# Sample rows of a hybrid decoder step: attention and state products in halves of 64 columns, and one state update for eight rows

## The chip, the cores and the metric

One Trainium2 chip, of which the kernel uses one core. The metric is the device time of one launch in microseconds (us). A core has a matrix engine (PE, whose weight loads are listed apart as PEld), a vector engine (DVE), a scalar engine (ACT), GpSimd (POOL) and a queue engine (SP) from which nearly all of this kernel's DMAs are issued. Each engine works through its own instructions in order.

## What is computed

One trunk layer for a prompt of 2048 tokens and for a sample batch of 8 rows with 8 new tokens each (64 sample tokens). The layer is: RMSNorm, one input projection, two groups of heads side by side, one output projection, then a squared-ReLU MLP. All inputs are float32. What matters here are the two sample parts:

```python
def swa_window(q, k_all, v_all, sinks):           # 8 q heads, 2 kv heads, head size 64
    scores = jnp.einsum('bqhgd,bkhd->bhgqk', qg, k_all) * (HEAD_DIM ** -0.5)
    p = sink_softmax(scores, mask, sink)          # 128 cached keys + the new ones
    out = jnp.einsum('bhgqk,bkhd->bqhgd', p, v_all)

def step(S, xs):                                  # GLA, 4 heads, dk 64, dv 128
    qd, kd, vv, ab = xs
    o = jnp.einsum('bthk,bhkv->bthv', qd, S)      # the state's read-out
    S = ab[..., None] * S + jnp.einsum('bthk,bthv->bhkv', kd, vv)
```

For the sample batch the scan has one step: all 8 new tokens of a row form one chunk. The state `S` of a row and head is 64 x 128, so that two heads (a head group `g`) fill 128 partitions.

## The kernel before

**Stages.** The kernel projects the attention columns and does the attention tile by tile (16 prompt tiles of 128 tokens, then the sample tile, whose index is `NB` = 16), then the GLA part tile by tile, then the output projection, then the MLP. The columns of the GLA part are projected by `projecting` (products `gproj`, each 128 x 128 weights with 384 moving columns), which serves as fill: the loops draw a given number of its products between the steps of the latency-bound work, so that PE always has something in its queue.

**Sample attention** (`sample_unit`, line 564). There are four units, one for each half `c` of the sample rows and each kv head `r`. A unit makes scores `sc` (128 rows: 4 sample rows x 4 heads x 8 tokens; 192 columns: 128 cached keys and the 64 new ones), the softmax in the tile `s` (tag `ss`, two buffers), two transposes into `pt`, two copies by DVE into `pc`, and the product with the values into the bank `av`: one product with the new values `vals[NB]` (64 partitions, 128 moving columns) and four with the cached values (32 moving columns each). Each uses all 128 columns of the values, that is of both kv heads, and only the half `av[rr]` of the result that belongs to head `r` is copied out. `vals[NB]` is written in `take_rest` (line 362).

**Sample GLA** (`gla_sample`, line 1306). It is a generator, called `side` in the main loop, and takes one step whenever the GLA loop over the prompt tiles (`gla`, line 1214) yields: five turns for each prompt tile, from tile 1 on. The part that matters is the last one. It first makes the inner product `oi` (four products, 128 columns of the values, 64 moving columns). Then for each head group `g`:

- the read-out `oe`: 8 products, one for each row `b`, whose weights are the state `s0[:, b]` (128 x 128) and whose moving operand has 16 columns;
- the decay of the state: one DVE multiplication over 128 x 1024 elements;
- the update, in four steps of two rows each (`b2`), each a turn of the side generator: two masked copies of the keys (`s_kx`, one for each row, by DVE), then a yield, then four products of 64 x 64 weights and 128 moving columns into a bank `ds`, and one DVE addition of 256 columns to the state;
- the state is written out by a DMA; after the first group the state of the second is loaded into the same place, and the generator passes `S_WAIT[1]` = 6 turns.

After the second group it transposes and normalizes the result (`finish_out`), and frees the pool `ss`; then `split_wo` (line 1425), which prepares the output weights in eight steps, one for each prompt tile, takes its place.

**PSUM.** `bank` (line 178) gives the kinds `a`, `b` and `c` two buffers each, `d` and `e` one. All of the side generator's products go to kind `b`.

**Records.** A float32 product that is not a transpose appears in the trace as two matmul records (with two weight loads), so the 8 products of one group's read-out are 16 records. A transpose, and a product of the type fp32r (`gproj`), is one record. The instructions of each engine need not stand in the order of the source: the first masked copies of the keys, for instance, stand far ahead of the read-out.

Of the kernel before, what the change touches and what calls it, by code (L numbers as in the profile page):

```python
# [12 lines left out]
F32 = mybir.dt.float32  # L13
# [3 lines left out]
ALU = mybir.AluOpType  # L17
# [4 lines left out]
P = 128  # L22
D = 1024
KT = D // P
T = 2048
NB = T // P
DB, DT = 8, 8
NS = DB * DT
W = 128
HD = 64  # L30
# [13 lines left out]
SL = len(S_LEVELS)  # L44
# [108 lines left out]
def hybrid_step_kernel(ctx: ExitStack, tc: tile.TileContext, I, O):  # L153
    nc = tc.nc
# [18 lines left out]
    te, ac, dv = (InOrder(tc, engine) for engine in (nc.tensor, nc.scalar, nc.vector))  # L173
# [4 lines left out]
    def bank(shape, kind, name):  # L178

        return ps.tile(shape, F32, tag=kind, name=name, bufs=1 if kind in "de" else 2)  # L180
# [21 lines left out]
    ident = cpool.tile([P, P], F32, name="ident")  # L202
# [79 lines left out]
    sp = open_pool("a_s")  # L282
    gxTs, ropes, xs_in, xTs, proj, qks, rots, heads, vals = {}, {}, {}, {}, {}, {}, {}, {}, {}
# [69 lines left out]
    def scaled(out, i, src):  # L353
        ac.activation(out, src, AF.Copy, scale=rstd_all[: rows(i), i : i + 1])
# [7 lines left out]
    def take_rest(i):  # L362

        n = rows(i)
        p_ = proj.pop((i, 1))
        w = 640 - A_N
        scaled(qks[i].rearrange("p h d -> p (h d)")[:n, A_N:640], i, p_[:n, :w])
        vps = p_[:n, w : w + P]
        rs = rstd_all[:n, i : i + 1]
        gps_ = p_[:n, w + P : A_N]  # L370
        ranks = glr[:n, i // 2, i % 2, :48].rearrange("p (a r) -> p a r", a=3)
        scaled(ranks[:, 0:3:2], i, gps_.unsqueeze(1).to_broadcast([n, 2, 16]))

        def low(out, src, hi):
            dv.scalar_tensor_tensor(out, src, rs, f32(hi), op0=ALU.mult, op1=ALU.subtract)

        if i == NB:
            vals[i] = vn = sp.tile([NS, P], F32, tag="vv", name="vn", bufs=4)
            scaled(vn, i, vps)
            return lambda: low(ranks[:, 1], gps_, ranks[:, 0])  # L380
        vals[i] = vv = sp.tile([P, 2, 2, HD], F32R, tag="vv", name=f"vv_{i}", bufs=4)
        vh, vl = vv[:, :, 0, :], vv[:, :, 1, :]
        src = vps.rearrange("p (r d) -> p r d", r=2)
        scaled(vh, i, src)
        if i == NB - 1:
            vo = sp.tile([P, P], F32, tag="kc", name="vo", bufs=1)
            scaled(vo, i, vps)
            stores.append((O["v_win_prompt"][0, 0].rearrange("w h d -> w (h d)"), vo))

        def lows():  # L390
            low(vl, src, vh)
            low(ranks[:, 1], gps_, ranks[:, 0])

        return lows
# [26 lines left out]
    half_of = slice(HD), slice(HD, P)  # L421
# [142 lines left out]
    def sample_unit(c, r, cached, kcs, mo):  # L564

        yield
        qs, kns = heads[NB]
        rr = slice(r * HD, (r + 1) * HD)
        if r == 0:
            pc = bank([P, 4, P], "d", f"pc_{c}")  # L570
            for b in range(4):
                te.transpose(pc[:, b, :], cached["k", c][:, b, :], ident)
            kcs[c] = sp.tile([P, 4, P], F32, tag="kc", name=f"kc_{c}", bufs=1)
            ac.activation(kcs[c], pc, AF.Copy)
        kc = kcs[c]
        yield
        sc = bank([P, W + NS], "b", f"ssc_{r}_{c}")
        for b4 in range(4):
            b = c * 4 + b4
            lq = qs[rr, b].rearrange("p j t -> p (j t)")  # L580
            o_ = slice(b4 * 32, b4 * 32 + 32)
            te.matmul(sc[o_, :W], lq, kc[rr, b4, :], start=True, stop=True)
            te.matmul(sc[o_, W:], lq, kns[rr, :], start=True, stop=True)
        s = sp.tile([P, W + NS], F32, tag="ss", name=f"ss_{r}_{c}", bufs=2)
        m = sp.tile([P, 1], F32, tag="sm", name=f"sm_{r}_{c}", bufs=2)
        yield
        dv.tensor_tensor_reduce(
            s, sc, smask[:, c, :], scale=1.0, scalar=sinkp[:, r : r + 1], op0=ALU.add, op1=ALU.max, accum_out=m
        )
        neg = sp.tile([P, 1], F32, tag="sneg", name=f"sneg_{r}_{c}", bufs=2)  # L590
        dv.tensor_scalar(neg, m, -1.0, None, op0=ALU.mult)
        es = sp.tile([P, 1], F32, tag="ses", name=f"ses_{r}_{c}", bufs=2)
        den = sp.tile([P, 1], F32, tag="sden", name=f"sden_{r}_{c}", bufs=2)
        ac.activation(es, sinkp[:, r : r + 1], AF.Exp, bias=neg)
        ac.activation(s, s, AF.Exp, bias=neg, accum_out=den)
        yield
        dv.tensor_tensor(den, den, es, op=ALU.add)
        dv.reciprocal(den, den)
        dv.tensor_scalar(s, s, den, None, op0=ALU.mult)
        yield  # L600
        pt = bank([P, 2, P], "c", f"spt_{r}_{c}")
        te.transpose(pt[:, 0, :], s[:, :W], ident)
        te.transpose(pt[:NS, 1, :], s[:, W:], ident)
        yield
        pc = sp.tile([P, 2, P], F32, tag="spc", name=f"spc_{r}_{c}", bufs=2)
        dv.tensor_copy(pc[:, 0, :], pt[:, 0, :])
        dv.tensor_copy(pc[:NS, 1, :], pt[:NS, 1, :])
        yield
        av = bank([P, P], "e", f"sav_{r}_{c}")
        te.matmul(av, vals[NB], pc[:NS, 1, :], start=True, stop=False)  # L610
        for b4 in range(4):
            o_ = slice(b4 * 32, b4 * 32 + 32)
            te.matmul(av[:, o_], cached["v", c][:, b4, :], pc[:, 0, o_], start=False, stop=b4 == 3)
        yield
        dv.tensor_copy(
            mo[rr, :, c * 32 : c * 32 + 32].rearrange("p j (b t) -> p b j t", b=4),
            av[rr].rearrange("p (b j t) -> p b j t", b=4, j=4),
        )
        if (c, r) == (1, 1):
            stores.append((mix_d[NB][:, 0:4, :], mo))  # L620
        yield
# [245 lines left out]
    kcs, cached = {}, {}  # L867
# [158 lines left out]
    sp = open_pool("g_s")  # L1026
# [21 lines left out]
    ss = open_pool("g_sam")  # L1048
# [2 lines left out]
    s_dec = ss.tile([P, SL + 1, 2, NS], F32, name="s_dec")  # L1051
    s_kd = ss.tile([NS, 256], F32, name="s_kd")
    s_kdT = ss.tile([P, 2, NS], F32, name="s_kdT")
    s_xk = ss.tile([P, SL, 2, NS], F32, name="s_xk")
    s_xq = ss.tile([P, SL, 2, 2, NS // 2], F32, name="s_xq")
    s_qz = ss.tile([P, 2, 2, NS], F32, name="s_qz")
    s_kt = ss.tile([P, 2, NS], F32, name="s_kt")
    s_before, s_after = (ss.tile([P, 2, NS], F32, name=f"s_{name}") for name in ("before", "after"))
    s_at = ss.tile([NS, 4, NS], F32, name="s_at")
    s_oT = ss.tile([P, 4, NS], F32, name="s_oT")  # L1060
    s_sg = ss.tile([NS, 512], F32, name="s_sg")
    s_kx = ss.tile([NS, 2, P], F32, name="s_kx")
    for u in range(2):
        nc.vector.memset(S[u], 0.0)
    nc.gpsimd.memset(qz, 0.0)
# [240 lines left out]
    def gla_sample(gp):  # L1306

        i = NB
        state = I["state_gla"][0].rearrange("b (g h) k v -> g (h k) b v", g=2)
        s0 = s0_place  # L1310
# [25 lines left out]
        yield  # L1336
        oi = bank([P, 4, NS], "b", "s_oi")
        for h in range(4):
            te.matmul(oi[:, h, :], gv[:, h * P : (h + 1) * P], s_at[:, h, :], start=True, stop=True)
        nc.scalar.activation(s_oT, oi, AF.Copy)  # L1340
        for g in range(2):
            oe = bank([P, 2, NS], "b", f"s_oe{g}")
            for b in range(DB):
                bb = slice(b * DT, (b + 1) * DT)
                te.matmul(oe[:, :, bb], s0[:, b, :], s_qz[:, :, g, bb], start=True, stop=True)
            nc.vector.tensor_tensor(s_oT[:, 2 * g : 2 * g + 2], s_oT[:, 2 * g : 2 * g + 2], oe, op=ALU.add)
            full = s_dec[:, SL, g].rearrange("p (b t) -> p b t", t=DT)[:, :, DT - 1 : DT]
            nc.vector.tensor_tensor(s0, s0, full.to_broadcast([P, DB, P]), op=ALU.mult)
            for b2 in range(DB // 2):
                for u in range(2):  # L1350
                    hot = onehot[:, b2 * 2 + u : b2 * 2 + u + 1]
                    nc.vector.tensor_scalar(s_kx[:, u], s_kd[:, g * P : (g + 1) * P], hot, None, op0=ALU.mult)
                yield
                ds = bank([P, 2, P], "b", f"sds_{g}_{b2}")
                for u in range(2):
                    for r, rr in enumerate(half_of):
                        h = 2 * g + r
                        te.matmul(ds[rr, u], s_kx[:, u, rr], gv[:, h * P : (h + 1) * P], start=True, stop=True)
                dst = s0[:, b2 * 2 : b2 * 2 + 2, :]
                nc.vector.tensor_tensor(dst, dst, ds, op=ALU.add)  # L1360
            nc.sync.dma_start(O["gla_sample"][0, :, 2 * g : 2 * g + 2].rearrange("b h k v -> (h k) b v"), s0)
            if g == 0:
                nc.sync.dma_start(s0, state[1])
                for _ in range(S_WAIT[1]):
                    yield
# [1048 lines left out]
```

## Time and profile before

| | us |
|---|---|
| three timed runs | 2161.69, 2162.13, 2163.29 (median 2162.13) |
| the profiled execution | 2162.71 |
| its span, first to last instruction | 2160.9 |
| PE busy | 2149.6 (99%) |
| DVE busy | 1529.1 (71%) |
| ACT busy | 1221.6 (57%) |
| POOL busy | 258.5 (12%) |
| sample attention, four units | about 281 to 311 of the span |
| sample GLA, from the inner product to the last state update | about 374 to 449 of the span |

The span is followed from the last instruction back to what released it; this chain of waits, listed in order of time, has for each piece its start, its length, its engine and tile, and how many instructions it merges. A granted clock of 1 means that the TensorE clock was not throttled. In the lists of instructions, the tile written stands ahead of `<-` and those read stand behind it; the counts of the form "128*64 128x64" give the rows and columns of the weights and the partitions and columns of the moving operand. The state tile `s0` is listed under the name `s`, `av` of the sample units as `sav`, `ds` of the sample as `sds`, `oi` and `oe` as `s_oi` and `s_oe`; `gl` and `ds` are products of the prompt's GLA that have similar shapes.

### The profile page before, as it was taken

The page shows a single profiled execution, that of the slowest core. Times are in us where ns is not written, and L with a number is a line of the kernel's source. Part 1 is how long each engine was busy: PE and PEld are TensorE (multiplying, and loading weights), DVE is VectorE, ACT ScalarE, POOL GpSimd, SP SyncE. Part 2 cuts the span into 40 slices and gives each one's busy share as a digit, 9 for nine tenths or more (in the row PEclk, how much of TensorE's full clock was granted, in tenths as well). Part 3 has the DMA queues.
Part 4 walks back from the last instruction along what each step waited for, and adds up shares of the span by engine and source line. Part 5 has one row for each costly group of instructions (what it writes and reads, how often), then busy time and mean ns, then how long its engine had stood idle before and what let it go on. Part 6 is the DMA issues. An engine that isn't in the chain of part 4 may idle for free.

```text
span 2160.9 us, 34240 instructions
## 1 busy us (share of the span) xinstructions
PE 2149.6 (99%) x11799; PEld 1864.0 (86%) x11799; DVE 1529.1 (71%) x3203; ACT 1221.6 (57%) x2625; POOL 258.5 (12%) x417
## 2 busy tenths in 40 slices
PE   9999999999999999999999999999999999999998
PEld 9999999999998888888888888888888888888887
DVE  7999868777775766988888545547766666555566
ACT  7999867566664444655555544445454445444454
POOL 4676511111111100000000000000000000000000
PEclk9999999999999999999999999999999999999999
DMA  7444341234338566777785777668544443766685
GB/s 242 154 147 148 99 117 40 71 106 135 136 126 270 199 216 220 245 269 274 256 279 208 269 247 223 208 199 274 183 171 155 157 150 126 257 203 195 195 267 181
DMA packets 241322, 411.54 MB, mean 190 GB/s; under 512 B 24876, under 2 KB 143132, under 8 KB 237036
## 3 DMA queue, kind: packets, MB, share of 16 engines
q1 hardware_dynamic: 240988, 409.08, 57.1%
q8 instruction: 93, 1.52, 0.3%
q14 instruction: 81, 0.66, 0.1%
q10 hardware_dynamic: 160, 0.27, 0.0%
HBM read 265.82 MB, written 143.99 MB: 190 GB/s over the span
## 4 chain that ended last, share of the span: by engine, by line
PE 93%; DVE 2%; ACT 2%; DMA 1%; issue 1%; POOL 0%; SPq 0%; DVEq 0%; POOLq 0%; ACTq 0%
PE dn L142 27%; PE gproj L142 13%; PE uc L142 8%; PE uX L142 8%; PE out L1419 7%; PE proj L142 6%; PE ue L142 4%; PE ud L142 4%; PE ub L142 4%; PE dsam L142 1%; PE sam L142 1%; PE o L142 1%; PE sc L142 1%; PE pT L142 1%; PE av L142 1%; PE out L142 1%
## 5 line engine op out<-in xcount | busy, mean ns | idle before, releaser
L142 PE MATMUL dn<-o1t,o0s 128*128 128x512 f32 x892 | 347.9, 390 | 0.8 <-DVE o1t L229 0.8
L142 PE MATMUL dn<-o0t,o1s 128*128 128x512 f32 x892 | 347.7, 390 | 0.0
L142 PE MATMUL dn<-o0t,o0s 128*128 128x512 f32 x892 | 347.4, 389 | 0.3 <-DVE f L2075 0.3
L229 DVE TENSOR_TENSOR o1s<-rs,o0s 128x512 fp32r<-128x512 f32 x224 | 154.6, 691 | 220.8 <-ACT o0s L228 218.5
L228 ACT ACTIVATE o0s<-rs 128x512 fp32r<-128x512 f32 x224 | 141.1, 631 | 291.9 <-PE dn L142 261.6
L142 PE MATMUL gproj<-wg,gxh 128*128 128x384 f32 x1024 | 273.2, 342 | 0.0
L142 PEld LDWEIGHTS dn<-o1t,o0s 128*128 128x128 f32 x892 | 167.4, 188 | 37.3 <-DVE o1t L229 1.7
L142 PEld LDWEIGHTS dn<-o0t,o0s 128*128 128x128 f32 x892 | 167.5, 188 | 36.8 <-DVE f L2075 0.7
L142 PEld LDWEIGHTS dn<-o0t,o1s 128*128 128x128 f32 x892 | 167.4, 188 | 35.2
L142 ACT ACTIVATE st<-st 128x512 f32<-128x512 f32 x224 | 141.1, 630 | 100.2 <-DVE st L142 95.1
L142 PEld LDWEIGHTS gproj<-wg,gxh 128*128 128x128 f32 x1024 | 184.2, 189 | 3.5 <-issue 3.1
L142 PE MATMUL uc<-H,s 128*128 128x512 f32 x768 | 186.5, 391 | 0.1
L142 PE MATMUL gproj<-wg,gxl 128*128 128x384 f32 x576 | 185.9, 340 | 0.0
L142 PE MATMUL uX<-H,w 128*128 128x512 f32 x768 | 185.2, 390 | 0.0
L142 PEld LDWEIGHTS uX<-H,w 128*128 128x128 f32 x768 | 144.0, 188 | 30.3
L142 PEld LDWEIGHTS uc<-H,s 128*128 128x128 f32 x768 | 143.0, 188 | 30.6 <-ACT st L142 0.3
L1419 PE MATMUL out<-wo,mt 128*128 128x512 f32 x680 | 158.6, 392 | 0.0
L229 DVE TENSOR_TENSOR o1t<-rt,o0t 128x512 fp32r<-128x512 f32 x223 | 152.7, 685 | 5.3 <-ACT o0t L228 3.7
L218 POOL TENSOR_TENSOR frs<-rs_v,half 128x1 f32<-128x1 f32 (+1 forms) x13 | 11.5, 891 | 1198.6 <-DVE rs_v L216 1198.6
L1419 PEld LDWEIGHTS out<-wo,mt 128*128 128x128 f32 x680 | 126.5, 188 | 26.1
L228 ACT ACTIVATE o0t<-rt 128x512 fp32r<-128x512 f32 x223 | 137.7, 618 | 7.5 <-DMA rt<-t_d 4.8
L142 DVE TENSOR_TENSOR st<-st 128x512 f32<-128x512 f32 x160 | 110.7, 692 | 30.1 <-ACT st L142 25.8
(429 smaller groups left out, 4307.2 us busy)
## 6 DMA issues: line engine op xcount, KB each, us to landing
s_d<-st SPq DMA_DIRECT2D x32, 1792.0 KB, 8.9
rs<-s_d SPq DMA_DIRECT2D x224, 256.0 KB, 3.0
raw<-in_w_up SPq DMA_DIRECT2D x64, 512.0 KB, 4.6
rt<-t_d SPq DMA_DIRECT2D x128, 256.0 KB, 3.9
rt<-in_w_down SPq DMA_DIRECT2D x96, 256.0 KB, 2.9
t<-in_w_down SPq DMA_DIRECT2D x64, 256.0 KB, 3.7
t_d<-t SPq DMA_DIRECT2D x32, 512.0 KB, 5.1
h_d<-ht SPq DMA_DIRECT2D x8, 1280.0 KB, 7.6
```

The lines of the kernel that those rows point to most:

```text
L142: ins = call(*a, **k)
L218: return nc.gpsimd.tensor_tensor(out, v[:n], e, op=ALU.pow)
L228: nc.scalar.activation(hi, src, AF.Copy)
L229: return vector.tensor_tensor(lo, src, f32(hi), op=ALU.subtract)
L1419: te.matmul(banks[c], x, w[:, c * 512 : (c + 1) * 512], start=k + u == 0, stop=k == KT - 1 and u == len(products) - 1,)
```

## The change

It touches three places.

In the sample attention the values of the new tokens become a tile of 128 partitions, whose upper half GpSimd fills with zeros. The softmax tile becomes 256 columns wide (in the ring of tag `s`, three buffers, which the prompt's units use too), and GpSimd fills its last 64 columns with zeros, so that both transposes are 128 x 128 and one DVE copy takes both. The products with the values use the 64 columns of head `r` alone and write `av[rr]`; the one with the new values has 128 partitions in place of 64.

In the sample GLA the inner product and the read-out become two products each of 64 columns, the two halves of the values going to the two halves of the partitions: 8 products in place of 4, and 16 in place of 8 for each group.

The state update makes one masked copy of the keys for all eight rows (one DVE multiplication with both operands broadcast), yields once, makes all 16 products into two banks, and adds each bank to the state with one DVE addition of 512 columns. The side generator so takes 3 turns fewer for each group, 6 in all. Five small tiles (`s_xk`, `s_xq`, `s_kt`, `s_before`, `s_kx`) share one work tile, so that `s_kx` has room for eight rows.

```diff
-            vals[i] = vn = sp.tile([NS, P], F32, tag="vv", name="vn", bufs=4)
-            scaled(vn, i, vps)
+            vals[i] = vn = sp.tile([P, P], F32, tag="vv", name="vn", bufs=4)
+            nc.gpsimd.memset(vn[NS:], 0.0)
+            scaled(vn[:NS], i, vps)
...
-        s = sp.tile([P, W + NS], F32, tag="ss", name=f"ss_{r}_{c}", bufs=2)
+        wide = sp.tile([P, 2 * P], F32, tag="s", name=f"ss_{r}_{c}", bufs=3)
+        nc.gpsimd.memset(wide[:, W + NS :], 0.0)
+        s = wide[:, : W + NS]
...
-        te.transpose(pt[:, 0, :], s[:, :W], ident)
-        te.transpose(pt[:NS, 1, :], s[:, W:], ident)
+        for u in range(2):
+            te.transpose(pt[:, u, :], wide[:, u * P : (u + 1) * P], ident)
...
-        dv.tensor_copy(pc[:, 0, :], pt[:, 0, :])
-        dv.tensor_copy(pc[:NS, 1, :], pt[:NS, 1, :])
+        dv.tensor_copy(pc, pt)
...
-        te.matmul(av, vals[NB], pc[:NS, 1, :], start=True, stop=False)
+        te.matmul(av[rr], vals[NB][:, rr], pc[:, 1, :], start=True, stop=False)
...
-            te.matmul(av[:, o_], cached["v", c][:, b4, :], pc[:, 0, o_], start=False, stop=b4 == 3)
+            te.matmul(av[rr, o_], cached["v", c][:, b4, rr], pc[:, 0, o_], start=False, stop=b4 == 3)
...
+    s_work = ss.tile([P, D], F32, name="s_work")
+    s_xk = s_work[:, :384].rearrange("p (l g k) -> p l g k", l=SL, g=2)
+    s_xq = s_work[:, 384:768].rearrange("p (l r g q) -> p l r g q", l=SL, r=2, g=2)
...
+    s_kt, s_before = (s_work[:, c : c + P].rearrange("p (g k) -> p g k", g=2) for c in (768, 896))
...
+    s_kx = s_work[:NS].rearrange("p (b k) -> p b k", b=DB)
...
-            te.matmul(oi[:, h, :], gv[:, h * P : (h + 1) * P], s_at[:, h, :], start=True, stop=True)
+            for u, uu in enumerate(half_of):
+                te.matmul(oi[uu, h, :], gv[:, h * P + u * HD : h * P + (u + 1) * HD], s_at[:, h, :], start=True, stop=True)
...
-                te.matmul(oe[:, :, bb], s0[:, b, :], s_qz[:, :, g, bb], start=True, stop=True)
+                for uu in half_of:
+                    te.matmul(oe[uu, :, bb], s0[:, b, uu], s_qz[:, :, g, bb], start=True, stop=True)
...
+            keys = s_kd[:, g * P : (g + 1) * P].unsqueeze(1).to_broadcast([NS, DB, P])
+            nc.vector.tensor_tensor(s_kx, keys, onehot.unsqueeze(2).to_broadcast([NS, DB, P]), op=ALU.mult)
...
-            for b2 in range(DB // 2):
-                for u in range(2):
-                    hot = onehot[:, b2 * 2 + u : b2 * 2 + u + 1]
-                    nc.vector.tensor_scalar(s_kx[:, u], s_kd[:, g * P : (g + 1) * P], hot, None, op0=ALU.mult)
-                yield
-                ds = bank([P, 2, P], "b", f"sds_{g}_{b2}")
-                for u in range(2):
-                    for r, rr in enumerate(half_of):
-                        h = 2 * g + r
-                        te.matmul(ds[rr, u], s_kx[:, u, rr], gv[:, h * P : (h + 1) * P], start=True, stop=True)
-                dst = s0[:, b2 * 2 : b2 * 2 + 2, :]
-                nc.vector.tensor_tensor(dst, dst, ds, op=ALU.add)
+            yield
+            states = [bank([P, 4, P], "b", f"sds_{g}_{c}") for c in range(2)]
+            for b in range(DB):
+                for r, rr in enumerate(half_of):
+                    h = 2 * g + r
+                    te.matmul(states[b // 4][rr, b % 4], s_kx[:, b, rr], gv[:, h * P : (h + 1) * P], start=True, stop=True)
+            for c in range(2):
+                dst = s0[:, c * 4 : c * 4 + 4, :]
+                nc.vector.tensor_tensor(dst, dst, states[c], op=ALU.add)
```

More of the change, by code (lines that the diff above doesn't have):

```diff
@@ L1053, in hybrid_step_kernel @@
     s_kdT = ss.tile([P, 2, NS], F32, name="s_kdT")
-    s_xk = ss.tile([P, SL, 2, NS], F32, name="s_xk")
-    s_xq = ss.tile([P, SL, 2, 2, NS // 2], F32, name="s_xq")
+    s_work = ss.tile([P, D], F32, name="s_work")
+    s_xk = s_work[:, :384].rearrange("p (l g k) -> p l g k", l=SL, g=2)
+    s_xq = s_work[:, 384:768].rearrange("p (l r g q) -> p l r g q", l=SL, r=2, g=2)
     s_qz = ss.tile([P, 2, 2, NS], F32, name="s_qz")
-    s_kt = ss.tile([P, 2, NS], F32, name="s_kt")
-    s_before, s_after = (ss.tile([P, 2, NS], F32, name=f"s_{name}") for name in ("before", "after"))
+    s_kt, s_before = (s_work[:, c : c + P].rearrange("p (g k) -> p g k", g=2) for c in (768, 896))
+    s_after = ss.tile([P, 2, NS], F32, name="s_after")
     s_at = ss.tile([NS, 4, NS], F32, name="s_at")
@@ L1061, in hybrid_step_kernel @@
     s_sg = ss.tile([NS, 512], F32, name="s_sg")
-    s_kx = ss.tile([NS, 2, P], F32, name="s_kx")
+    s_kx = s_work[:NS].rearrange("p (b k) -> p b k", b=DB)
     for u in range(2):
```

## The prediction

> **What bounds the kernel now.** I read the page first (busy times and shares of the chain), then the chain of waits in order of time over the two stretches that the change touches, then the granted clock by windows, and last the groups of single tiles.
>
> ```profile
> span 2160.9 us, 34240 instructions
> PE 2149.6 (99%) x11799; PEld 1864.0 (86%) x11799; DVE 1529.1 (71%) x3203; ACT 1221.6 (57%) x2625; POOL 258.5 (12%) x417
> PE 93%; DVE 2%; ACT 2%; DMA 1%; issue 1%; POOL 0%; SPq 0%; DVEq 0%; POOLq 0%; ACTq 0%
> ```
>
> PE carries 93% of the chain. Busy time says little about single products, since their ends overlap; the chain's pieces do not overlap, so I work with those:
>
> ```profile
> 284.68 0.61 DVE pl L142
> 285.33 0.58 PE av L142 x3
> ...
> 302.63 1.95 PE gproj L142 x10
> 304.58 1.42 PE sav L142 x10
> 306.00 2.34 PE gproj L142 x13
> ...
> 311.85 11.45 PE gproj L142 x66
> ...
> 368.09 0.84 PE sgm L142 x12
> 368.93 4.19 PE gproj L142 x23
> ...
> 374.14 1.03 PE s_oi L142 x8
> 375.18 2.07 PE s_oe L142 x16
> 377.24 1.47 PE gproj L142 x4
> 378.71 1.75 PE gl L142 x32
> ...
> 383.53 0.58 PE sds L142 x8
> 384.12 1.93 PE gproj L142 x10
> ...
> 404.01 1.08 PE gl L142 x32
> 405.78 0.44 PE ds L142 x8
> ...
> 424.91 1.69 PE s_oe L142 x16
> 426.60 0.79 PE gproj L142 x4
> ```
>
> After the DVE piece at 284.68 every piece up to the end of the sample's GLA is PE. So what a product of the sample takes there is paid in full, and what it gives up is won in full, as long as the others keep up. An undisturbed `gproj` takes 11.45 / 66 = 0.1735 us. What a block of small products costs is therefore its own piece plus what the `gproj` behind it take beyond 0.1735 each.
>
> **The sum, part by part.**
>
> *Values of the sample attention.* One unit now: 1.42 for its 10 records, and 2.34 - 13 x 0.1735 = 0.08 behind it, 1.50 us. Afterwards it has as many records with 64 columns of weights, all on the same half. The nearest row is `sgm`: 64 columns of weights, 64 moving columns, 0.84 for 12 records, 0.07 each, and 4.19 - 23 x 0.1735 = 0.20 behind it (leaving a mode with fewer columns costs more). Two of the ten have 128 moving columns; in `ds`, eight records with 128 take 0.44, in pairs on alternating halves, so 0.11 for each of a half, 0.05 more than `sgm`'s 0.06 (0.84 less an entry of 0.14, worked out below, over 12). Afterwards: 10 x 0.07 + 2 x 0.05 + 0.20 = 1.00 us. Won: 0.50 a unit, **2.0 us** for four. Bounds: 0, if a load of 64 columns takes as long as one of 128 behind a full array; 3.4, if records go by at the 0.034 of `gl` below.
>
> *Inner product and read-out.* The products change from 128 columns to pairs on alternating halves, twice as many. `gl` has that very shape (128 rows, 64 columns, halves in turn): 1.08 for 32 records, 0.034 each, entry included. The inner product goes from 1.03 for 8 records to 16 x 0.034 = 0.54: 0.49 won. The read-out of the second group goes from 1.69 plus 0.79 - 4 x 0.1735 = 0.10 behind it to 32 x 0.034 = 1.08 plus 0.20: 0.51 won, and the same for the first. Together **1.5 us**. That the moving operand has 16 columns and `gl` 64 I leave out: the read-out's pace today does not follow the moving columns, as its 0.105 a record lies close to the 0.11 of `ds` with 128.
>
> *State update.* Eight blocks of 0.58 plus 1.93 - 10 x 0.1735 = 0.20 behind each make 6.2 us. Afterwards there are two blocks of 32 records: four times the 0.44 of `ds`, an entry of 0.58 - 0.44 = 0.14, and 0.20 behind, 2.1 each, 4.2 together. Won: **2.0 us**. The products are the same; six entries and exits go.
>
> *The clock.* The first read-out's pieces are longer than the second's: 2.07 against 1.69, then four `gproj` 1.47 against 0.79, then `gl` 1.75 against 1.08, 1.73 in all. The windows say why:
>
> ```profile
> 373.32:376.73 3.41, 3.41 (x29) 3.10 (x27) 2.37 (x9) 2.65 (x9) 0.00 (x0) 1.00 0.00 0
> 376.73:380.14 3.41, 3.41 (x35) 2.97 (x37) 1.42 (x2) 1.43 (x5) 0.00 (x0) 0.50 0.35 90
> ```
>
> (columns: the stretch and its length, busy time of PE, PEld, DVE, ACT and POOL, granted clock, DMA.) For 3.41 us the clock was granted at 0.50, right behind a stretch filled by the inner product and the read-out, 3.1 us of small products in a row. Half of 3.41 is the **1.7 us**. Afterwards that row is 0.54 + 1.08 plus entries and exits, under 2 us, and `gproj` fill the rest of any such stretch; I take it that the window does not come. Bounds: 0 won, if it still comes; 1.7.
>
> [...]
>
> *DVE, ACT, POOL, SP.* DVE's share by groups:
>
> ```profile
> L1352 DVE TENSOR_SCALAR s_kx<-s_kd,c x16: 270/272/1107, 367.7 to 447.0; 64x128 f32<-64x128 f32 x16
> L1348 DVE TENSOR_TENSOR s<-s,s_dec x2: 1219/1223/1227, 377.3 to 427.6; 128x1024 f32<-128x1024 f32 x2
> L1360 DVE TENSOR_TENSOR s<-s,sds x8: 400/406/412, 384.6 to 450.6; 128x256 f32<-128x256 f32 x8
> L142 DVE COPY spc<-spt x8: 271/280/293, 290.2 to 308.8; 128x128 f32<-128x128 f32 x4, 64x128 f32<-64x128 f32 x4
> ```
>
> For each group eight masks of 0.27 and four additions of 0.41 (3.8 us) become one mask over 1024 elements (1.22, by the decay's row, which has two operands of that length) and two additions of at most twice 0.41 (1.6). DVE gains 1 us a group, and a copy in each attention unit; none of it is on the chain, so I count nothing. What may matter is when the mask runs:
>
> ```profile
> 367.74 0.47 DVE L1352 TENSOR_SCALAR s_kx<-s_kd,c 64x128 f32<-64x128 f32 x2
> ...
> 380.51 1.58 DVE L1163 COPY_PREDICATED AH<-c,gl 128x128 f32<-128x128 uint8 x4 [1.81 <-PE gl L142]
> 382.20 0.64 DVE L1163 COPY_PREDICATED AH<-c,gh 128x128 f32<-128x128 uint8 x2
> 382.88 0.29 DVE L1274 COPY AT<-AH 64x256 f32<-64x256 f32 x1
> 383.20 0.61 DVE L1280 SCALAR_TENSOR_TENSOR S<-S,dec,ds 128x128 f32<-128x128 f32 x2
> ```
>
> Today the first two masks stand long before the read-out. The new one cannot: it lies in the place of `s_xk` and `s_xq`, which `sgm` reads until 368.93. It fits into the 1.81 us that DVE waits for `gl` at 378.7 to 380.5, so I price it at nothing; without that cover see the second rival. The two additions stand ahead of nothing that PE awaits within some 4 us.
>
> ```profile
> 302.81 0.53 POOL L1065 MEMSET qz<- 128x512 f32 x1 [30.52 <-ACT wg L142]
> 385.16 0.31 POOL L1211 MEMSET after<- 128x256 f32 x1 [12.75 <-ACT kdT L1136]
> 402.72 0.39 SPq L1361 DMA_DIRECT2D out_gla_sample<-s  x1
> 405.96 0.38 SPq L1363 DMA_DIRECT2D s<-in_state_gla  x1
> 406.62 0.34 SPq L626 DMA_DIRECT2D gxh<-xt_d  x1
> ```
>
> The four fills of the softmax tile are a quarter of the 256 columns that took 0.31, and POOL idles for 30.5 us there; the fill of the values, at most 0.31, comes before 270, where POOL also rotates the sample's heads; I take 0 between 0 and 0.3. The first group's store waits for its additions at the head of SP's queue, and the reload 3.2 us more behind it, so that the load of `gxh` stands behind both. They move three turns earlier, away from the `gxh` load at 406.62, and six turns still separate reload and second read-out: nothing. `split_wo` begins a prompt tile sooner; nothing waits for it before the last tile: nothing.
>
> **Sum:** 2.0 + 1.5 + 2.0 + 1.7 = 7.2 us, 2162.71 - 7.2 = **2155.5 us** (the profiled execution has 1.8 us outside its span, and lies 0.6 above the median of 2162.13). The bound between faster and no change, 0.2%, about what can be told apart here, is 4.3 us below that median, 2157.8. If the slow window came in the runs before only now and then, or comes again, the time is 2157.2, still on the faster side.
>
> **Rivals.**
>
> *Halves do not overlap.* If a pair on two halves takes its two weight loads one after the other, inner product and read-outs go at `sgm`'s 0.07: 16 x 0.07 = 1.12 (0.09 lost), 32 x 0.07 + 0.20 = 2.44 against 1.79 (0.65 lost, twice), 1.4 lost in place of 1.5 won, and the slow window stays, since the row of small products is no shorter. 2162.7 - 4.0 + 1.4 = 2160.1. Against it: `gl` with its 0.034. For it: nothing shows `gl` with so few moving columns. [...]
>
> *PE waits for the mask.* If it stands behind the copies above, it runs from 383.8 to 385.0, while PE wants the products at 383.53: 1.5 us for each group, 3.0, giving 2158.5. For it: the copies belong to the prompt's own chain and are ready as soon as `gl` ends. Against it: DVE waits idle just ahead of them.
>
> *The same wait, and slower.* One place further back, the mask would stand behind a prompt tile's level sums:
>
> ```profile
> 370.95 0.32 DVE L1156 TENSOR_TENSOR after<-after,before 128x128 f32<-128x128 f32 x1
> ...
> 376.23 0.29 DVE L1157 TENSOR_TENSOR before<-before 128x128 f32<-128x128 f32 x1
> ```
>
> These take 5.6 us with ACT in turn. 1.5 + 5.6 = 7.1 for each group is 14.2 against 7.2 won: 2169.7. It decides from 3.6 us a group. Against it: in the profile these sums end at 376.5, before the read-out does.
>
> **Chances.** The forecast, 2154 to 2157.8, 0.68. Halves without overlap 0.10; wait for the mask, short, 0.10; a sum that comes out smaller by sizes alone (the two bounds at 0), 2157.8 to 2160, 0.05: these three within 0.2%, 0.25. The long wait 0.07, slower. The range goes from 2153.0 (values at 0.034, 1.4 us more, against the median) to 2160.8, which takes in all but the long wait.
>
> **What would show it.** `sav` at about 0.8 in the chain; `s_oe` at 1.1 twice, with 32 records; two `sds` pieces of 1.9; granted clock 1.00 from 370 to 390; no piece of DVE between 285 and 450. Wrong would be: `s_oe` above 1.7, a wait of `sds` for `s_kx`, or a window at 0.50.

## The result, and the profile after

| | before | after |
|---|---|---|
| median of the timed runs, us | 2162.02 (2161.39 to 2163.29, 6 runs) | 2154.32 (2153.55 to 2154.93, 6 runs) |
| ratio | | 0.9964, 95% interval 0.9954 to 0.9973 |
| span of the profiled execution, us | 2160.9 | 2152.6 |

The kernel is 7.7 us faster by the medians (5.8 to 9.9 by the interval). The forecast was 2155.5. The chain of waits of the changed kernel, in order of time (start, length, engine and tile, instructions merged):

```profile
283.80 0.57 PE av L142 x3
...
302.13 0.80 PE sav L142 x10
302.93 2.45 PE gproj L142 x13
...
307.80 0.58 PE gqk L142 x4
...
365.03 0.84 PE sgm L142 x12
...
371.09 0.61 PE s_oi L142 x16
371.70 1.04 PE s_oe L142 x32
372.74 0.89 PE gproj L142 x4
373.63 1.08 PE gl L142 x32
...
377.77 1.89 PE sds L142 x32
379.66 1.94 PE gproj L142 x10
...
397.21 1.08 PE gl L142 x32
...
408.30 1.04 PE s_oe L142 x32
...
414.38 1.89 PE sds L142 x32
...
487.78 1.08 PE gl L142 x32
```

Each of the sample's products is where the forecast had it: `sav` 0.80 where it was 1.42, both read-outs 1.04 where they were 2.07 and 1.69, and two blocks of `sds` of 1.89 in place of eight of 0.58. The four `gproj` behind the first read-out take 0.89 (four times 0.1735 and an exit of 0.20) and the `gl` its ordinary 1.08: the clock did not fall, as its window (columns as in the prediction, with GB/s last) says too:

```profile
366.00:384.00 18.00, 18.00 (x216) 16.79 (x216) 14.03 (x35) 8.25 (x28) 3.78 (x3) 1.00 0.32 97
```

To see where the time came from I compare the starts of pieces that both chains have. These are the ones of before that the prediction did not show:

```profile
311.38 0.47 PE gqk L142 x4
...
496.14 1.08 PE gl L142 x32
```

| the same piece | before | after | lead of after | won since the line above |
|---|---|---|---|---|
| last `av` of the prompt | 285.33 | 283.80 | 1.53 | |
| `gqk` behind the four attention units | 311.38 | 307.80 | 3.58 | 2.05 |
| `sgm` | 368.09 | 365.03 | 3.06 | -0.52 |
| `gl` of the fourth prompt tile | 404.01 | 397.21 | 6.80 | 3.74 |
| `gl` of the eighth prompt tile | 496.14 | 487.78 | 8.36 | 1.56 |

Two lines were not foreseen. The lead of 1.53 us at 284 lies ahead of the first product that the change touches. And 0.52 us is given back between `gqk` and `sgm`. Of this, 0.11 is the exit of the last `sav`, which falls on `gqk` (0.58 in place of 0.47). The other 0.41 is a new wait in the first prompt tile of the GLA: 30 `gproj` took 5.26 before, and now take 4.91 + 0.17 + 0.59.

```profile
320.00 4.91 PE gproj L142 x28
324.91 0.17 issue
325.07 0.59 PE gproj L142 x2
```

PE gets there earlier and finds ACT behind (waits of the changed kernel: who waited for whom, us in total, times, longest). The first of these two lines existed before, with 0.3 at most; the second did not.

```profile
PEld ssc L142 <- ACT kc L142: 0.5, 1, 0.5
PEld gproj L142 <- ACT dec L1156: 0.5, 1, 0.5
```

From 284 on the change is worth 8.36 - 1.53 = 6.83 us, against the 7.2 of the sum. I call the distance from the last `av` to this eighth `gl` **the stretch**: 210.81 before, 203.98 after. It is a better measure than a median here: single runs of one kernel spread by 1.4 to 8.5 us, while the stretch of the kernel before came out as 210.81 and 210.79 in its two profiles, and that of the changed kernel as 203.98 and 203.84.

### The profile page after: what moved, and what is told of

Same layout as the page of the kernel before. It is cut to its first block, busy times and chain, and to the rows that moved or that the text cites. A ratio compares the mean times of both kernels' runs of the same rounds, so it can differ in the third digit from the quotient of the medians.

```text
span 2152.6 us, 34310 instructions
## 1 busy us (share of the span) xinstructions
PE 2142.3 (100%) x11839; PEld 1859.7 (86%) x11839; DVE 1527.4 (71%) x3181; ACT 1219.5 (57%) x2625; POOL 260.0 (12%) x422
## 4 chain that ended last, share of the span: by engine, by line
PE 97%; ACT 1%; DVE 1%; DMA 1%; issue 0%; DVEq 0%; SPq 0%; ACTq 0%
PE dn L142 27%; PE gproj L142 13%; PE uc L142 8%; PE uX L142 8%; PE out L1423 7%; PE proj L142 6%; PE ue L142 4%; PE ud L142 4%; PE ub L142 4%; PE sam L142 2%; PE dsam L142 1%; PE sc L142 1%; PE pT L142 1%; PE o L142 1%; PE av L142 1%; PE out L142 1%
```

## The experiments

### The parts alone, and the kernel before once more

Three kernels make one edit each in the kernel before, in the form that the diff shows; a fourth is the kernel before unchanged.

> Kernel before with the attention edit alone (zero fill, 128 x 128 transposes, values' products of 64 columns). Theory (the sum by products): 2.0 us faster than before, sav pieces of 0.8 in the chain, the slow window still there or not as in the kernel before. Rival (the gain is the clock window's or the earlier turns'): within 0.5 us of before.

> Kernel before with inner product and read-out in halves alone. Theory: 1.5 us faster by the products, and up to 1.7 more where the kernel before has its window at clock 0.50 and this one has not: 1.5 to 3.2. Rival (the change's gain sits in the state update and the six turns that go): no more than the 1.5.

> Kernel before with the state update for eight rows alone (one mask, two banks, six turns fewer; the shared work tile too). Theory: 2.0 us faster, two sds pieces of 1.9, and the slow window as in the kernel before. Rival (the earlier turns bring more than the products): 3 us or more faster, with the surplus in gproj stretches that no product of the sample touches.

> The kernel before, unchanged. It tells how far two executions of one kernel lie apart ahead of 284 us of the span, where before and after differ by 1.5 us, and whether the window at clock 0.50 comes each time. Theory: same time within 0.5 us, and stretches ahead of 284 us that wander by 1 us or so. Rival (the first 284 us are made faster by the change): they stand within 0.2 us of the first profile of before.

| kernel | median (11 runs each) | ratio to before, 95% | stretch | won in the stretch | window at 0.50 |
|---|---|---|---|---|---|
| before, timed beside these | 2162.66 (33 runs) | | | | |
| attention alone | 2160.39 | 0.9991 (0.9982 to 1.0001) | 209.20 | 1.6 | yes |
| inner product and read-out alone | 2159.01 | 0.9983 (0.9975 to 0.9992) | 207.53 | 3.3 | no |
| state update alone | 2159.17 | 0.9985 (0.9976 to 0.9994) | 208.80 | 2.0 | yes |
| before again | 2162.34 | 1.0000 (0.9991 to 1.0009) | 210.79 | 0.0 | yes |

(Where one end of the stretch is not on the chain, its start is read from the timeline: the last `av` of the attention alone and of the pairs below, the eighth `gl` of the split row below.) The three parts add up: 1.6 + 3.3 + 2.0 = 6.9 us in the stretch, against 6.8 for the whole change, so nothing here shows that one part depends on another. The medians, with intervals of some 2 us to either side, say no more than that they agree.

The read-out alone wins 3.3, about the 1.5 of its products and the 1.7 of the clock together; the two shares are not quite these, see the part on the clock below. That no other part takes the window away can be seen in the windows of the other three kernels (columns as in the prediction), of the attention alone:

```profile
371.79:375.20 3.41, 3.41 (x28) 3.26 (x28) 1.66 (x5) 2.25 (x9) 0.00 (x0) 1.00 0.00 0
375.20:378.61 3.41, 3.41 (x56) 3.16 (x56) 1.98 (x5) 0.51 (x1) 0.00 (x0) 0.50 0.71 225
```

of the state update alone:

```profile
376.20:379.61 3.41, 3.41 (x60) 3.41 (x58) 3.17 (x9) 1.12 (x4) 0.00 (x0) 0.50 0.83 264
```

and of the kernel before in its second profile:

```profile
375.78:379.19 3.41, 3.41 (x46) 2.97 (x47) 1.63 (x3) 1.03 (x4) 0.00 (x0) 0.50 0.53 155
```

These windows start behind the read-out, and its piece is nevertheless longer than the 1.69 of the second group. It is 1.89 in all three kernels; in the chain of the attention alone:

```profile
371.73 1.03 PE s_oi L142 x8
372.76 1.89 PE s_oe L142 x16
```

The attention alone wins 1.6 in the stretch, not 2.0: the wait of the first GLA tile is there too.

The second profile of before settles the lead ahead of 284 us:

```profile
283.98 0.57 PE av L142 x3
```

The same kernel is 1.35 us earlier there than in its first profile (285.33). In all thirteen profiles this start lies between 283.37 and 285.33, earliest in two kernels without the edit of the attention. The first 284 us differ from execution to execution, and nothing puts the 1.53 us down to the change.

### Halves in turn, or one half after the other

> The changed kernel with the read-out's 16 products of a group ordered half by half: the lower half of the partitions for all eight rows, then the upper half. Same products, same counts. Theory (products on alternating halves overlap, those behind one another on one half don't): the read-out's records go from 0.033 to sgm's 0.06 to 0.07 each, its pieces from 1.04 to about 2.0, 1.9 us slower than the changed kernel for two groups, and 1.7 more if the longer row of small products brings the window at clock 0.50 back. Rival (64 columns are faster by themselves, in any order): pieces of 1.0 to 1.2, no difference.

```diff
-            for b in range(DB):
-                bb = slice(b * DT, (b + 1) * DT)
-                for uu in half_of:
+            for uu in half_of:
+                for b in range(DB):
+                    bb = slice(b * DT, (b + 1) * DT)
                     te.matmul(oe[uu, :, bb], s0[:, b, uu], s_qz[:, :, g, bb], start=True, stop=True)
```

The chain of this kernel:

```profile
371.89 0.61 PE s_oi L142 x16
372.50 1.76 PE s_oe L142 x32
374.27 0.90 PE gproj L142 x4
```

The same 32 records take 1.76 in place of 1.04, 0.055 each in place of 0.033, and the stretch is 205.31, 1.33 longer than the changed kernel's: two times 0.72, nearly. The weight loads show the same, all 32 of a read-out, in the changed kernel and then here:

```profile
371.63 1.01 PEld L142 LDWEIGHTS s_oe<-s_qz,s 128*64 128x64 f32 x32
...
372.43 1.73 PEld L142 LDWEIGHTS s_oe<-s_qz,s 128*64 128x64 f32 x32
```

So the gain of the read-out comes from the two halves alternating; twice as many products of 64 columns, one half after the other, cost as much as those of 128 columns before (1.69). The window did not come back with the longer row (0.61 + 1.76 = 2.4 us): the four `gproj` behind it take 0.90 and the `gl` 1.08, against 0.89 and 1.08 in the changed kernel. So in this one profile 2.4 us of small products did not bring it, while the 2.9 us of before (1.03 + 1.89) did. The median is 2156.71 in 8 runs, 0.9976 of before (0.9966 to 0.9987).

### The zero fill

> The changed kernel without the zero fill in the attention: values of the new tokens with 64 partitions, softmax tile of 192 columns in its own ring, second transpose of 64 columns, two copies; the products keep their 64 columns. Theory (the 64 columns bring the gain, the fill only spares a change of mode within the unit): sav pieces of 0.9 to 1.0 in place of 0.8, 0.4 to 0.8 us in all. Rival (the fill and the single copy bring the gain): sav pieces of 1.2 or more.

The edit undoes the lines of the diff that widen `vn` and the softmax tile, and the transposes and copies with them; the products keep `[rr]`. A piece of its chain:

```profile
303.03 0.94 PE sav L142 x10
303.97 2.12 PE gproj L142 x11
```

`sav` is 0.94 in place of 0.80, four times 0.14, and the stretch is 204.47, 0.49 longer. The 64 columns bring the attention's gain, and the zero rows a quarter of it: a product with 64 partitions ahead of products with 128 goes with 0.14 us more a unit. (Median 2156.41 in 7 runs, 0.9972 of before, 0.9962 to 0.9983.)

### The six turns

> The changed kernel with three idle turns behind each state update, so that the side generator takes as many turns as before. Theory (turns bring nothing): within 0.5 us of the changed kernel's 2154.3. Rival (finishing six turns earlier is part of the gain): 1 us or more slower.

```diff
                 nc.vector.tensor_tensor(dst, dst, states[c], op=ALU.add)
+            for _ in range(3):
+                yield
```

The stretch is 204.68, 0.70 longer than the changed kernel's (median 2156.41 in 6 runs, 0.9976 of before, 0.9964 to 0.9987). All its products have the changed kernel's lengths. What is new is one wait, in the sixth prompt tile:

```profile
PEld o L142 <- ACT AT L1278: 0.8, 1, 0.8
```

By 0.7 this is between what the two theories expected. The timeline shows what holds ACT up (an entry in brackets: how long the engine was idle, and until what):

```profile
445.62 0.25 ACT L1183 ACTIVATE ojunk<-s_ob 64x128 bf16<-64x128 f32 x1
...
447.19 0.16 DVE L216 TENSOR_SCALAR rs_v<-ossq 64x4 f32<-64x4 f32 x1 [1.82 <-ACT ojunk L1183]
447.27 1.58 DVE L1166 COPY_PREDICATED AH<-c,gl 128x128 f32<-128x128 uint8 x4
```

ACT's four sums of squares of the sample's result (`s_ob`) start at 445.6. DVE waits 1.82 us for them with `rs_v` at the head of its instructions, and the prompt's copies `AH`, on which `AT` and then PE's `o` depend, stand behind it. In the changed kernel the same `rs_v` runs at 422.7, before `gl` is done, and delays nothing. So the turns bring nothing by themselves, but where the sample's work falls can cost a wait; in the changed kernel it falls where none arises.

### Breaking up the row of small products

> The kernel before with one turn put between the inner product and the first read-out, so that gproj stand between them. No product changes. Theory (3 us of small products in one row bring the window at clock 0.50): no such window, s_oi 1.0 and s_oe 1.7 as before, about 1.7 us faster than before. Rival (the window comes from something else there, or belongs to the products themselves wherever they stand): the window stays, no difference.

```diff
         nc.scalar.activation(s_oT, oi, AF.Copy)
+        yield
         for g in range(2):
```

This is an edit of the kernel before. Its chain shows the products unchanged, but apart (behind `gproj` the first read-out takes 1.69, as the second does), and the windows show a full clock:

```profile
373.34 1.03 PE s_oi L142 x8
374.37 0.89 PE gproj L142 x4
375.27 1.08 PE gl L142 x32
...
379.40 1.69 PE s_oe L142 x16
```

```profile
366.00:384.00 18.00, 18.00 (x170) 16.91 (x169) 13.82 (x40) 10.89 (x31) 2.91 (x3) 1.00 0.23 76
```

The stretch is 209.23, 1.6 us shorter than before, with no product changed. But the time that was expected did not come: the median is 2161.97, 1.0001 of before (0.9992 to 1.0009). Right behind the stretch the trace has a wait that the kernel before has not:

```profile
PEld ds L142 <- ACT kd L1143: 1.0, 1, 1.0
```

By the next prompt tile 1.0 of the 1.6 us is gone again. So the theory of the window holds in this one trace, and its gain was mostly lost to one wait. The sample's later work runs a turn later here; whether this is what makes ACT late was not followed. The rest of 0.6 us is below what the medians can tell.

### Eight masks in place of one

> The changed kernel with eight masked copies of the keys, one for each row, in place of the one; turns, banks and products as changed. Theory (the mask is off the chain): DVE 1 us busier for each group, sds pieces and time as in the changed kernel, within 0.5 us. Rival (the single copy is what lets the products start in time): PE waits for DVE ahead of sds, 1 us or more slower.

```diff
-            keys = s_kd[:, g * P : (g + 1) * P].unsqueeze(1).to_broadcast([NS, DB, P])
-            nc.vector.tensor_tensor(s_kx, keys, onehot.unsqueeze(2).to_broadcast([NS, DB, P]), op=ALU.mult)
+            for b in range(DB):
+                nc.vector.tensor_scalar(s_kx[:, b], s_kd[:, g * P : (g + 1) * P], onehot[:, b : b + 1], None, op0=ALU.mult)
```

The stretch is 203.83, and the median 2155.31 beside 2155.06 of the changed kernel. The one masked copy brings nothing, for the two `sds` pieces are 1.90 and 1.89 without it too; what shortens `sds` is that all 16 products stand in one block. In the changed kernel the mask takes what the sum gave it, and it runs early:

```profile
L1353 DVE TENSOR_TENSOR s_work<-s_kd,c x2: 1209/1222/1235, 367.2 to 381.1; 64x1024 f32<-64x1024 f32 x2
```

The first starts at 367.2, ten microseconds ahead of its products, the second at 381.1, more than thirty ahead.

### Two heads' values together, and the changed kernel once more

> The changed kernel with the values' products of the two kv heads of a half of the rows made together, in the second of the two units: 10 products of 64 columns on alternating halves, twice, in place of 5 on one half, four times; one DVE copy for both. Theory (pairs overlap): two sav pieces of about 1.0 (four records with 128 moving columns at 0.055, sixteen at 0.034, entry 0.14) in place of four of 0.8, 1.8 us less with two exits spared. But in the first prompt tile of the GLA PE already waited 0.5 us for ACT in the changed kernel; if that wait takes the place of what is won, it grows to about 2 us and the net is under 0.5 us. Rival (the wait was accidental): the full 1.8 us.

> The changed kernel, unchanged, as the base for the two others of this call and for the offset of the first 284 us. Theory: 2154 to 2155.5, no window at clock 0.50, 6.8 us against before from 284 us on. Rival (the window comes in some executions here too): a profile with a window, or times that spread by 1.7 us more than those of before.

The edit holds the first head's `pc` back, and makes both heads' products in the second unit:

```diff
-        av = bank([P, P], "e", f"sav_{r}_{c}")
-        te.matmul(av[rr], vals[NB][:, rr], pc[:, 1, :], start=True, stop=False)
+        kcs["p", c, r] = pc
+        if r == 0:
+            yield
+            yield
+            return
+        av = bank([P, P], "e", f"sav_{r}_{c}")
+        for q, qq in enumerate(half_of):
+            te.matmul(av[qq], vals[NB][:, qq], kcs["p", c, q][:, 1, :], start=True, stop=False)
         for b4 in range(4):
             o_ = slice(b4 * 32, b4 * 32 + 32)
-            te.matmul(av[rr, o_], cached["v", c][:, b4, rr], pc[:, 0, o_], start=False, stop=b4 == 3)
+            for q, qq in enumerate(half_of):
+                te.matmul(av[qq, o_], cached["v", c][:, b4, qq], kcs["p", c, q][:, 0, o_], start=False, stop=b4 == 3)
         yield
-        dv.tensor_copy(
-            mo[rr, :, c * 32 : c * 32 + 32].rearrange("p j (b t) -> p b j t", b=4),
-            av[rr].rearrange("p (b j t) -> p b j t", b=4, j=4),
-        )
+        dv.tensor_copy(
+            mo[:, :, c * 32 : c * 32 + 32].rearrange("p j (b t) -> p b j t", b=4),
+            av.rearrange("p (b j t) -> p b j t", b=4, j=4),
+        )
```

```profile
295.63 0.81 PE sav L142 x20
...
305.63 0.81 PE sav L142 x20
```

Twice the records in the same 0.81: pairs on two halves cost what one half cost alone (1.0 was expected). The median is 2153.32 (5 runs), 0.9959 of before (0.9945 to 0.9972), beside 2155.06 of the changed kernel unchanged (5 runs, 0.9963, 0.9951 to 0.9976; stretch 203.84, no window). The stretch is 202.11, 1.87 shorter than the changed kernel's 203.98. This is the shortest of the kernels measured, but the intervals of the two ratios overlap, so the trace shows the gain and the times only fit it.

The wait that I expected to eat the gain is not there: in the first GLA tile PE waits for nothing. Another has grown in its place, from 0.5 in the changed kernel's first profile and 0.3 in its second to

```profile
PEld ssc L142 <- ACT kc L142: 1.1, 1, 1.1
```

so the expectation was wrong: the stretch wins the rival's full 1.8. Two `sav` pieces with their exits, 2.0 us, are gone, 0.6 us of PE's time goes to the wait that grew, and the 0.4 us of the wait that went come back.

## Why the prediction was right

**The bound.** That PE alone sets the pace from 285 to 450 held but for short waits for ACT: at 294 (`kc`), where the weight loads wait 0.5 us and the chain is 0.1 us longer than before, and at 325 (`dec`), which costs 0.4 us.

**Values of the attention.** Forecast 1.00 a unit with its exit; measured 0.80 + (2.45 - 13 x 0.1735 = 0.19) = 0.99. So the products won the 2.0 us, and the two waits for ACT took 0.5 of them. The sum had no term for PE outrunning ACT there; this gap accounts for the difference between 7.2 and 6.8.

**Inner product and read-out.** Forecast 0.54 and 1.08; measured 0.61 and 1.04. That the moving operand is narrower than `gl`'s made no difference, as taken (0.033 a record with 16 moving columns, `gl`'s 0.034 with 64). What was off is the first read-out before: the forecast gave it the second's 1.69, but right behind the inner product it takes 1.89 with the granted clock still at 1.00. So this part won 0.42 + 0.75 + 0.55 = 1.7 us, not 1.5.

**State update.** Forecast two blocks of 2.1 with exits; measured 1.89 + (1.94 - 10 x 0.1735 = 0.20), the same.

**The clock.** The window was laid to the row of small products, and this holds: the read-out alone removes it, and the split row removes it without changing a product (clock 1.00 from 366 to 384 in both). All four profiles in which the old inner product and read-out stand together have it, and the next `gl` takes 1.75 to 1.91. In the other nine that `gl` takes 1.08, and in the changed kernel the clock is below 1.00 only behind the last product of the program (0.77 from 2146.0 to 2152.6).

Its price was 1.5 us, not 1.7. The 1.73 of the forecast took in the 0.20 by which the first read-out is longer in any case; what is left in the first profile is 0.18 + 0.68 + 0.67, and the other three profiles give 1.5 to 1.6. The 0.2 that the clock has too much is what the read-out has too little, so the two errors cancel in the sum.

The window starts 2.6 us after the inner product's start in the first profile of before and 3.0 in the second, 3.5 and 3.8 in the others, so in these four it stands at no fixed distance from the row. What sets the distance was not shown.

An old row without the window did not come up in four profiles, but it seems to in timed runs. By an estimate from the profiles a whole window takes 0.0008 off the mean granted clock of an execution (half of 3.41, 1.7 of 2160 us), so an execution with a mean of 1.000 had none. This mean stands in 10 of 98 timed runs of the kernels with the old row (6 of 76 of the kernel before), and in 15 of 63 without it; a mean of 0.998 stands in 17 of the 98 and in none of the 63. So the window belongs to the row; by this estimate it comes in many executions and not in all, and how often is open. The medians of before mix the two.

**The mask, DVE and the turns.** They cost nothing, as priced, but for the mask the reason given was wrong. It does not sit in DVE's idle 1.8 us ahead of the six copies: it is free as soon as `sgm` is done, at 365.9, and runs at 367.2. Both rivals that made PE wait for it had no ground. The turns were priced at nothing because loads and stores had room. Two kernels show what that left out: with the sample's work moved by a few turns, one has a new wait of 0.8 us, traced to that work, and the other one of 1.0, whose origin is open.

**The rival of halves that do not overlap** fell with the read-out's 1.04; half by half it is 1.76. Both halves use all 128 rows in either order (weights 128 x 64), so what decides between 1.04 and 1.76 is whether consecutive products go to different halves.

**The size.** 2155.5 was forecast and 2154.3 measured. The sum was made from the first profile of before, and the 6.83 us of the stretch would have given 2155.9 from it. The remaining 1.5 us belong to the first 284 us, which wander by that much: that the time came out below the forecast, and not just above it, is luck. The lower end of the range, 2153.0, is 0.5 below what its own terms give (2162.13 - 7.2 - 1.4 = 2153.5).

## What to carry to other kernels

Where PE is the bound, look at what sets the pace of small float32 products. Here it was the columns of the weights (0.106 us a record at 128, 0.055 at 64 on one half), and not the moving columns from 16 to 64 (0.033 with 16 and 0.034 with 64, on alternating halves; `sds`, with 128 of them and 64 rows, takes 0.059). Then split the columns into two halves and let consecutive products alternate between them, and gather blocks of such products, because an entry and an exit together cost some 0.3 us here (0.14 and 0.20 for `sds`, the entry an estimate, 0.58 - 0.44). Leave out the half that nobody reads, as the values' product of the attention did. Price a block by a block of the same shape elsewhere in the same chain, its exit included; all four sizes came out within 0.1 us that way. Then ask at the next place where PE meets the other engines whether it now comes too early: what was won there can end in a wait a few microseconds on, and the same goes for work that merely moves to another turn.

## What was not expected of the hardware

Splitting the read-out's products into two halves won nothing by itself here: 32 records of 64 columns, one half after the other, took 1.76, as long as 16 of 128 columns (1.69), and only in alternation 1.04. And 2.9 us of small products in one row came with a clock of 0.50 for 3.41 us in each of four profiles, with PE busy in all of the 3.41 us ahead, while a row of 2.4 us did not in the one profile that has it. In at least 6 of 76 timed runs of the kernel before it did not come either, by the estimate from their mean clock of 1.000.
